# All four down entries of a group ahead of the first chunk in seven products

## The chip, the cores and the metric

The kernel runs on one core of one Trainium2 chip. The core has five engines that run side by side, each with its own in-order list of instructions: TensorE (PE, with its weight loads shown as PEld), VectorE (DVE), ScalarE (ACT), GpSimd (POOL) and SyncE (SP), which issues the loads here. The metric is the device time of one execution in microseconds (us).

## What is computed

The reference is a trunk of two decoder layers on a sequence of 512 tokens of width 1024. Each layer has a gated feed-forward block, a mixer (gated linear attention in layer 0, stick-breaking attention in layer 1) and a second feed-forward block, so that there are four feed-forward blocks (FFNs 1 to 4 below), each with a hidden width of 2816. All in float32.

```python
def swiglu(h, w_gate, w_up, w_down):
    return (jax.nn.silu(h @ w_gate) * (h @ w_up)) @ w_down

for i in range(DEPTH):                                   # DEPTH = 2
    x = x + 0.5 * swiglu(rmsnorm(x, ffn1_norm[i]), ...)  # FFN 1, FFN 3
    x = x + mixer_i(rmsnorm(x, mix_norm[i]))
    x = x + 0.5 * swiglu(rmsnorm(x, ffn2_norm[i]), ...)  # FFN 2, FFN 4
```

## The kernel before

**Numbers as pairs.** Every operand of a matmul is split in two parts: a high part in a shorter format, cast on ACT (`wh`, `hh`, `nh`, `th`), and the rest, the difference on DVE (`wl`, `hl`, `nl`, `tl`). A product is then three matmuls: high by high, low by high, high by low. So each chunk of weights costs, beside its load on SP's queue, one cast on ACT (line 138) and one subtraction on DVE (line 139), and these need free `wh` and `wl` buffers, of which there are four of each.

**Entries and the feed.** The work of TensorE is a list of entries (class `Entry`, line 108), each with the weights that it needs and a body that emits its matmuls and what takes their results. `Feed.start` (line 146) runs the entries in order; before an entry's matmuls it asks for the split of the weights of up to three entries and for the loads of up to six, beginning with its own. What this writes down is an order of the program; a scheduler then orders the instructions of each engine, by its own estimate of times, within what depends on what. Buffers come from pools; a new tile waits for the last user of the buffer that it gets. Raw weights have two buffers (`raw`), raw down weights two of their own (`rawd`).

**An FFN.** Class `FFN` (line 607) cuts the hidden width into 11 chunks of 256 columns, and the chunks into six groups, `GROUPS` in line 614: (0, 1), (2, 3), (4, 5), (6, 7), (8), (9, 10). A group's hidden tiles (two tiles of 128 rows for each chunk; t, cut into `hh` and `hl` by `close`) are multiplied by the down weights later, among the entries of the next group.

- Chunks 0 and 1 use plain products (`feat`, tile `ps_f`), a gate and an up entry for each half chunk, eight entries. The last two call `evac_u` (lines 853 and 854) for the last hidden tiles.
- From chunk 2 on (`SEVEN` = 2) gate and up are made by `seven` (line 684) in seven products of half size in place of eight, with sums and differences of the weight's quarters (tiles `s`, lines 694, 695, 700 and 701, on DVE) and of the input's. Each is two entries, with tiles `ps_w`, `ps_q` and `ps_z`. Seven groups of 12 matmuls of 256 columns follow each other: w, q, w again, z, and then w, q and w once more. Between the first and the third, ACT must copy `ps_w` to `ps_z` (line 736), since the third goes on in `ps_w`. Later ACT copies u from `ps_w` (line 754), DVE adds it (line 755) and adds to the second half (line 759), and for a gate ACT takes the silu (line 719).
- Below, G2 is the gate of chunk 2 in seven products, U2 its up, and so on; each has 84 matmuls.
- The input's sums (`sums`, line 833) are eight pieces of a cast to `th` (ACT, line 806) and a low part `tl` (DVE, line 807). They are spread over the entries that come before G2.
- The down entries of a group are made by `down` (line 312, tile `ps_d`, 24 matmuls of 512 columns). Those of the first group, chunks 0 and 1, are called D0 to D3 here, one for each 256 output columns; each ends in two additions to x on DVE (line 339). D0 is told `late`: it multiplies the three hidden tiles that are there first, and the fourth last. Groups 1 and 3 have their down products in seven as well (`seven_down`, lines 348 and 384).

**Where D0 to D3 stand.** The constructor of `FFN` lays out the list. At the start of group 1 it puts the first `AHEAD` of the four down entries (line 615: `NORMED, SEVEN, AHEAD = 6, 2, 2`), and the others between the entries of the group:

```python
                if group == 1:
                    for put in range(self.AHEAD):
                        down(*downs[put], late=put == 0)
                    put = self.AHEAD
                ...
                    while c >= self.SEVEN and put < len(downs) * (i + 1) // slots:
                        down(*downs[put])
                        put += 1
```

So the list was: eight entries of chunks 0 and 1, D0, D1, G2, U2, G3, D2, U3, D3, G4, U4 and so on. `sums_by`, the place of G2 in the list, is worked out from it, and `run` (line 902) spreads the first five of the sums' pieces over the entries from the seventh to G2, with `spread(todo[:5], self.sums_by - self.NORMED)`; the rest come behind the first entry of G2.

Of the kernel before, what the change touches and what calls it, by code (L numbers as in the profile page):

```python
# [46 lines left out]
def decoder(ctx: ExitStack, tc: tile.TileContext, a: dict, out: bass.AP):  # L47
# [559 lines left out]
    class FFN:  # L607
# [4 lines left out]


        GROUPS = ((0, 2), (2, 4), (4, 6), (6, 8), (8, 9), (9, 11))
        NORMED, SEVEN, AHEAD = 6, 2, 2
        DOWN_SEVEN = (1, 3)
        SEVEN_UP = (2, 3, 4, 5, 6, 7, 8, 9, 10)

# [698 lines left out]
    class SB:  # L1317
# [5 lines left out]
        AHEAD = 5  # L1323
# [582 lines left out]
```

## Time and profile before

| | |
|---|---|
| median of 3 runs | 1781.29 us (1780.68 to 1782.69) |
| the profiled execution | 1780.26 us, its span 1778.3 us |
| TensorE busy | 1760.1 us, 99% of the span, 12714 matmuls |
| weight loads (PEld) busy | 1631.7 us, 92% |
| VectorE busy | 1538.5 us, 87% |
| ScalarE busy | 1050.5 us, 59% |
| granted clock of TensorE | 1.000 |
| DMA | 179.24 MB, mean 101 GB/s |

A row of a timeline gives the start in us from the span's beginning, the duration, the engine, the line, the operation and its tiles (out<-in), the shape and how many were merged; in brackets stands the idle time of the engine before it and what ended it. Matmuls overlap each other, and their ends are modelled: what a matmul costs is read from the distance of the starts, not from its duration. The rows of the waits give who waited for whom, the total in us, the times and the longest. In the first FFN D0 begins at about 54 us and G2 at 64 us; G2 begins at about 611 us in FFN 2, 936 us in FFN 3 and 1497 us in FFN 4.

### The profile page before, as it was taken

How to read it: one execution, taken by the hardware profiler on the slowest of the kernel's cores; microseconds unless marked ns; L12 is line 12 of the kernel's file. 1: busy time of each engine (PE TensorE's matmuls, PEld its weight loads, DVE VectorE, ACT ScalarE, POOL GpSimd, SP SyncE). 2: the span in 40 equal slices, each digit the busy share in tenths (PEclk: the TensorE clock that was granted, in tenths of full speed). 3: DMA queues.
4: the chain of work that ended last, by engine and by line, in shares of the span. 5: the costliest groups of instructions: out<-in, count | busy, mean ns of one | idle time of the engine just before them, and what ended most of it. 6: DMA issues, size and time to landing. Idle time of an engine off the chain costs nothing.

```text
span 1778.3 us, 31182 instructions
## 1 busy us (share of the span) xinstructions
PE 1760.1 (99%) x12714; PEld 1631.7 (92%) x12714; DVE 1538.5 (87%) x2527; ACT 1050.5 (59%) x1830; POOL 9.8 (1%) x24
## 2 busy tenths in 40 slices
PE   9999999999999999999999999999999999999998
PEld 8999999889888899999889999999888888999997
DVE  8999798786878999889798988977898679998986
ACT  7556455554655556555555555655888755565554
POOL 0000000100000000000000000000000000000000
PEclk9999999999999999999999999999999999999999
DMA  5433334322122333333333333322212233333331
GB/s 167 142 115 112 107 96 132 93 71 72 49 95 95 104 110 119 107 107 108 109 93 119 96 119 103 124 84 83 83 48 72 71 95 119 110 105 111 105 126 52
DMA packets 178755, 179.24 MB, mean 101 GB/s; under 512 B 4082, under 2 KB 170276, under 8 KB 178612
## 3 DMA queue, kind: packets, MB, share of 16 engines
q1 hardware_dynamic: 177760, 175.91, 31.6%
q8 instruction: 99, 1.62, 0.4%
q0 software_dynamic: 608, 1.05, 0.2%
q14 instruction: 44, 0.36, 0.1%
q10 hardware_dynamic: 244, 0.29, 0.0%
HBM read 175.17 MB, written 2.10 MB: 100 GB/s over the span
## 4 chain that ended last, share of the span: by engine, by line
PE 64%; DVE 25%; ACT 7%; issue 3%; DMA 1%; SPq 0%; DVEq 0%; ACTq 0%
PE ps_w L709 14%; PE ps_d L80 12%; PE ps_f L80 8%; DVE wl L139 7%; PE ps_q L709 7%; PE ps_t L80 5%; PE ps_z L709 3%; PE ps_b L80 3%; ACT wh L138 3%; PE ps_w L384 2%; DVE x L390 2%; DVE ts L816 1%; PE ps_q L384 1%; PE ps_z L1394 1%; DVE xn L800 1%
## 5 line engine op out<-in xcount | busy, mean ns | idle before, releaser
L139 DVE TENSOR_TENSOR wl<-raw,wh 128x1024 fp32r<-128x1024 f32 x241 | 254.9, 1058 | 58.1 <-ACT wh L138 57.5
L138 ACT CAST wh<-raw 128x1024 fp32r<-128x1024 f32 x241 | 221.6, 920 | 72.4 <-PE ps_f L80 21.5
L139 DVE TENSOR_TENSOR wl<-s,wh 128x1024 fp32r<-128x1024 f32 x176 | 214.2, 1217 | 42.2 <-ACT wh L138 41.9
L138 ACT CAST wh<-s 128x1024 fp32r<-128x1024 f32 x176 | 184.2, 1047 | 102.9 <-DVE s L701 25.7
L709 PE MATMUL ps_w<-th,wh 128*128 128x256 f32 x864 | 239.8, 278 | 3.7 <-ACT ps_z L736 2.7
L709 PE MATMUL ps_w<-th,wl 128*128 128x256 f32 x864 | 237.6, 275 | 0.0
L709 PE MATMUL ps_w<-tl,wh 128*128 128x256 f32 x864 | 237.6, 275 | 0.0
L709 PEld LDWEIGHTS ps_w<-th,wh 128*128 128x128 f32 x864 | 165.8, 192 | 7.4 <-ACT ps_z L736 7.1
L80 PE MATMUL ps_f<-xh,wh 128*128 128x512 f32 x432 | 166.8, 387 | 0.9 <-DVE x L260 0.9
L709 PEld LDWEIGHTS ps_w<-tl,wh 128*128 128x128 f32 x864 | 165.9, 192 | 0.0
L709 PEld LDWEIGHTS ps_w<-th,wl 128*128 128x128 f32 x864 | 165.8, 192 | 0.0
L80 PE MATMUL ps_f<-xh,wl 128*128 128x512 f32 x432 | 164.2, 380 | 0.5 <-DVE wl L139 0.5
L80 PE MATMUL ps_f<-xl,wh 128*128 128x512 f32 x432 | 164.0, 380 | 0.0
L80 PE MATMUL ps_d<-hl,wh 128*128 128x512 f32 x416 | 158.0, 380 | 0.9 <-DVE hl L807 0.8
L80 PE MATMUL ps_d<-hh,wh 128*128 128x512 f32 x416 | 157.7, 379 | 0.2 <-ACT hh L806 0.2
L80 PE MATMUL ps_d<-hh,wl 128*128 128x512 f32 x416 | 157.7, 379 | 0.0
L138 ACT CAST wh<-rawd 128x1024 fp32r<-128x1024 f32 (+1 forms) x100 | 82.9, 845 | 60.1 <-PE ps_d L80 45.2
L139 DVE TENSOR_TENSOR wl<-rawd,wh 128x1024 fp32r<-128x1024 f32 (+1 forms) x100 | 95.7, 961 | 14.7 <-ACT wh L138 14.7
L80 PEld LDWEIGHTS ps_f<-xh,wh 128*128 128x128 f32 x432 | 81.7, 189 | 12.1 <-DVE x L260 1.3
L80 PEld LDWEIGHTS ps_f<-xl,wh 128*128 128x128 f32 x432 | 81.7, 189 | 11.5
L80 PEld LDWEIGHTS ps_f<-xh,wl 128*128 128x128 f32 x432 | 81.7, 189 | 11.1 <-DVE wl L139 0.9
L339 DVE SCALAR_TENSOR_TENSOR x<-ps_d,x 128x512 f32<-128x512 f32 x120 | 79.8, 682 | 13.8 <-PE ps_d L80 13.7
(352 smaller groups left out, 5247.9 us busy)
## 6 DMA issues: line engine op xcount, KB each, us to landing
raw<-in_ffn_w_gate_dram SPq DMA_DIRECT2D x43, 1024.0 KB, 5.4
raw<-in_ffn_w_up_dram SPq DMA_DIRECT2D x43, 1024.0 KB, 5.3
rawd<-in_ffn_w_down_dram SPq DMA_DIRECT2D x84, 512.0 KB, 3.6
raw<-in_gla_w_in_dram SPq DMA_DIRECT2D x12, 1024.0 KB, 5.3
raw<-in_sb_w_in_dram SPq DMA_DIRECT2D x16, 512.0 KB, 3.7
raw<-in_gla_w_out_dram SPq DMA_DIRECT2D x4, 1024.0 KB, 5.2
raw<-in_sb_w_in_dram SPq DMA_DIRECT2D x4, 1024.0 KB, 5.0
raw<-in_sb_w_out_dram SPq DMA_DIRECT2D x4, 1024.0 KB, 5.1
```

The source lines that it names most:

```text
L80: st["pe"] = nc.tensor.matmul(ps, l, r, start=first, stop=last).ins
L138: st["cut"] = nc.scalar.copy(h[:, k], part).ins
L139: nc.vector.tensor_tensor(out=l[:, k], in0=part, in1=h[:, k].bitcast(F32), op=ALU.subtract)
L339: nc.vector.scalar_tensor_tensor(out=x, in0=flat(ps), scalar=0.5, in1=x, op0=ALU.mult, op1=ALU.add)
L384: st["pe"] = nc.tensor.matmul(ps, l_, r_, start=first and c + n == 0, stop=c == 1 and n == 2, skip_group_check=True).ins
L390: nc.vector.scalar_tensor_tensor(out=x, in0=ps, scalar=0.5, in1=x, op0=ALU.mult, op1=ALU.add)
L709: st["pe"] = nc.tensor.matmul(o, l_, r_, start=first and j + n == 0, stop=j == 3 and n == 2, skip_group_check=True).ins
L800: nc.vector.scalar_tensor_tensor(out=t, in0=xs[k], scalar=g, in1=st["R"], op0=ALU.mult, op1=ALU.mult)
L816: nc.vector.tensor_tensor(out=o, in0=p, in1=q, op=ALU.subtract)
L1394: nc.tensor.matmul(o_, l_, r_, start=first, stop=last, skip_group_check=True)
```

## The change

`AHEAD` becomes 4, in the one class that all four FFNs use. All four down entries D0 to D3 stand ahead of G2; the loop among group 1's entries then has none left to put. `sums_by` becomes 12 where it was 10, and so the first five pieces of the input's sums are spread over six entries where it was four. Nothing is added or taken away: each engine has the same instructions in another order.

```diff
         GROUPS = ((0, 2), (2, 4), (4, 6), (6, 8), (8, 9), (9, 11))
-        NORMED, SEVEN, AHEAD = 6, 2, 2
+        NORMED, SEVEN, AHEAD = 6, 2, 4
         DOWN_SEVEN = (1, 3)
```

## The prediction

> **What bounds the kernel now.** I read the page first (busy shares), then busy time by stage, then the waits, then the starts of the matmuls, and last what ACT and DVE did ahead of each late start. The names D0 to D3, G2, U2, G3, U3, G4, U4 are those of the section on the kernel.
>
> ```profile
> 42.00:64.00 22.00, 21.93 (x100) 18.26 (x99) 22.00 (x34) 9.85 (x15) 0.00 (x0) 1.00 0.45 144
> 84.00:113.00 29.00, 29.00 (x218) 27.71 (x217) 26.86 (x46) 16.89 (x30) 0.00 (x0) 1.00 0.39 123
> PEld ps_w L709 <- ACT ps_z L736: 7.1, 18, 1.4
> ```
>
> The first two rows are stages of the first FFN: up to the first seven products, and from G3 to U3. The columns are length, then PE, PEld, DVE, ACT, POOL with their counts, the granted clock, the DMA share and GB/s. TensorE is busy in 21.93 of 22.00 and 29.00 of 29.00 us, at the full clock (1.00). So only starts that come late can be won or lost: the change removes no matmul. In the first stage DVE is busy 22.00 of 22.00 us: it works off the sums' splits and is second to PE. The last row, from the waits, names what holds PE in the seven products: the copy of `ps_w` into `ps_z` on ACT, 18 times.
>
> **What a late start costs, and where.** In a seven-product entry PE forms w, then q, then adds to w; ACT must have copied w to z by then. The last q and the first w of each place in the stretch that changes:
>
> ```profile
> 76.40 0.28 PE L709 MATMUL ps_q<-th,wl 128*128 128x256 f32 x1
> 76.52 0.28 PE L709 MATMUL ps_q<-tl,wh 128*128 128x256 f32 x1
> 76.95 0.38 PE L709 MATMUL ps_w<-th,wh 128*128 128x256 f32 x1 [0.16 <-ACT ps_z L736]
> 77.17 0.28 PE L709 MATMUL ps_w<-th,wl 128*128 128x256 f32 x1
> ...
> 124.82 0.28 PE L709 MATMUL ps_q<-tl,wh 128*128 128x256 f32 x1
> 125.26 0.38 PE L709 MATMUL ps_w<-th,wh 128*128 128x256 f32 x1 [0.16 <-ACT ps_z L736]
> ...
> 623.51 0.28 PE L709 MATMUL ps_q<-tl,wh 128*128 128x256 f32 x1
> 623.77 0.38 PE L709 MATMUL ps_w<-th,wh 128*128 128x256 f32 x1
> ...
> 671.64 0.28 PE L709 MATMUL ps_q<-tl,wh 128*128 128x256 f32 x1
> 672.08 0.38 PE L709 MATMUL ps_w<-th,wh 128*128 128x256 f32 x1 [0.16 <-ACT ps_z L736]
> ...
> 948.12 0.28 PE L709 MATMUL ps_q<-tl,wh 128*128 128x256 f32 x1
> 949.58 0.38 PE L709 MATMUL ps_w<-th,wh 128*128 128x256 f32 x1 [1.19 <-ACT ps_z L736]
> ...
> 1499.14 0.28 PE L709 MATMUL ps_q<-tl,wh 128*128 128x256 f32 x1
> 1499.68 0.38 PE L709 MATMUL ps_w<-th,wh 128*128 128x256 f32 x1 [0.26 <-ACT ps_z L736]
> ```
>
> Undisturbed starts are 0.11 apart (76.40 to 76.52). The wait at 76.95 pushes the start by 0.43 - 0.11 = 0.32, and the next one by 0.22 - 0.11 = 0.11 more: 0.43 lost for 0.16 of idle time. The same reading gives, by place: U2 0.43 (FFN 1), 0.26 (FFN 2), 1.46 (FFN 3), 0 (FFN 4), in all 2.15; G2 in FFN 4 0.54; U4 0.43 in FFN 1 and 0.44 in FFN 2, in all 0.87. U3, which today follows D2, shows none. The places where a U follows its G directly are the ones that lose. Why, in the worst one:
>
> ```profile
> 946.38 0.42 ACT L719 ACTIVATE o<-o 128x256 f32<-128x256 f32 x1 [2.94 <-DVE o L755]
> 948.22 1.03 ACT L138 CAST wh<-s 128x1024 fp32r<-128x1024 f32 x1
> 949.15 0.37 ACT L736 COPY ps_z<-ps_w 128x256 f32<-128x256 f32 x1
> ...
> 944.20 1.21 DVE L139 TENSOR_TENSOR wl<-raw,wh 128x1024 fp32r<-128x1024 f32 x1
> 945.93 0.41 DVE L755 TENSOR_TENSOR o<-u,o 128x256 f32<-128x256 f32 x1
> ```
>
> ACT had copied G2's u by 943.44 (946.38 less its idle 2.94), but DVE came to its add (L755) only at 945.93, being behind with splits and sums; ACT, in its written order, stood idle 2.94 us for it, and the z copy of U2 came last of all, at 949.15.
>
> **The change, part by part.**
>
> *TensorE's order.* In the built program each of the four FFNs now has D0 D1 D2 D3 G2 U2 G3 U3 G4, where it had D0 D1 G2 U2 G3 D2 U3 D3 G4; nothing else moves on PE, and the matmuls are the same. Work itself: 0. A down entry is 24 matmuls of 512 columns, 0.21 apart (1490.75 to 1490.96 in the fence on D0), 5.2 us; the two that move give DVE and ACT 10.4 us more before G2, and take these out of the run behind it.
>
> *DVE and ACT in front of G2.* D2's and D3's casts and splits and their four adds to x come earlier: 2 splits at 1.13 and 4 adds at 0.60 (spacing of the starts below) are 4.7 us of DVE for 10.4 us of PE. DVE thus gains 5.7 us on PE by the start of G2.
>
> So the late L755 at G2 goes away: in the new DVE order no sum or split that isn't needed by then stands directly ahead of it, and what stands ahead is finished while D3 runs. U2 loses between 0 and 0.43 (its smaller rows); I take 0, since the lag that made it is covered: -2.15. G2 of FFN 4 was late for the same lag: -0.54.
>
> *U3 and U4.* U3 now follows G3 directly, with the closing of U2 and one sum ahead of L755 on DVE: the same neighbours as U4 behind G4. Bounds: 0 (its own rows today) and 1.46 (U2 of FFN 3). Walking DVE down from G3's start (cuts of U2's output, 4.4 us; two sums 1.2; splits 0.6, 1.1, 1.1; a sum 0.6) L755 comes 9.1 us after it, when u has waited since 7.2, and z ends 2.72 us behind U3's start, where PE wants it at 2.68. Nearest is the row at 623.77: 0.26. Four times: +1.04. U4 keeps its neighbours: its 0.87 stays; bounds 0 and 4 x 0.44.
>
> *The last h of chunk 1, in D0.* D0 ends on the fourth hidden tile, whose cast (hh, ACT) and low part (hl, DVE) stand amid the moved splits.
>
> ```profile
> 1486.83 0.68 DVE L854 TENSOR_TENSOR t<-ps_f,t 128x512 f32<-128x512 f32 x1
> 1487.43 1.21 DVE L139 TENSOR_TENSOR wl<-s,wh 128x1024 fp32r<-128x1024 f32 x1
> ...
> 1489.69 0.68 DVE L807 TENSOR_TENSOR hl<-t,hh 128x512 fp32r<-128x512 f32 x1
> ...
> 1488.29 0.38 PE L80 MATMUL ps_d<-hl,wh 128*128 128x512 f32 x1
> 1488.90 0.48 PE L80 MATMUL ps_d<-hh,wh 128*128 128x512 f32 x1 [0.23 <-ACT hh L806]
> 1489.22 0.38 PE L80 MATMUL ps_d<-hh,wl 128*128 128x512 f32 x1
> 1490.43 0.48 PE L80 MATMUL ps_d<-hl,wh 128*128 128x512 f32 x1 [0.83 <-DVE hl L807]
> 1490.75 0.38 PE L80 MATMUL ps_d<-hh,wh 128*128 128x512 f32 x1
> 1490.96 0.38 PE L80 MATMUL ps_d<-hh,wl 128*128 128x512 f32 x1
> ...
> 56.44 0.68 DVE L807 TENSOR_TENSOR hl<-t,hh 128x512 fp32r<-128x512 f32 x1
> 58.12 0.38 PE L80 MATMUL ps_d<-hl,wh 128*128 128x512 f32 x1
> ...
> 604.68 0.68 DVE L807 TENSOR_TENSOR hl<-t,hh 128x512 fp32r<-128x512 f32 x1
> 605.42 0.48 PE L80 MATMUL ps_d<-hl,wh 128*128 128x512 f32 x1
> ...
> 929.29 0.68 DVE L807 TENSOR_TENSOR hl<-t,hh 128x512 fp32r<-128x512 f32 x1
> 930.02 0.48 PE L80 MATMUL ps_d<-hl,wh 128*128 128x512 f32 x1
> ```
>
> A short DVE instruction holds the engine 0.60 (1486.83 to 1487.43), a 1024-wide split 1.13 (two of them from 1487.43 to 1489.69). Counting these down the new order from the split of U1's weights, hl starts in FFN 1 1.10 later than today (its reader at 58.12 had 1.00 to spare): +0.25 with the restart. FFN 2: 0.64 earlier, where today the reader starts 0.06 behind hl's end, so waits for it: -0.3. FFN 3: 0.49 later with 0.05 to spare: +0.6. FFN 4: the same instant (two splits of D2 and D3 for the two of G2): 0. Together +0.55; bounds -1.8 (all of it hidden, with FFN 4's 0.4 + 1.0) and +2.4 (as FFN 4 in all).
>
> *Queues and waits.* D2's and D3's loads stand on SP's queue right behind U2's, as today; the next two, the down weights of the following stage, now pass G3's and wait for the splits of D2 and D3 (about 59 us), before G2's raw buffer comes free for G3's load (about 68). G3 is used at 94. No cost. The adds of D2 and D3 on DVE wait for PE; what is queued behind them is for U2 and later, more than 9 us off. On ACT hh now stands behind the cast of D2 (FFN 1, 2) or of D2 and D3 (FFN 3, 4), which wait for their loads:
>
> ```profile
> 51.84 2.71 SPq L105 DMA_DIRECT2D rawd<-in_ffn_w_down_dram  x2
> rawd<-in_ffn_w_down_dram SPq DMA_DIRECT2D x2, 512.0 KB, 3.9
> ```
>
> D0's split comes two short instructions (1.2 us) earlier, and so does the load: in FFN 4 D3's is issued at about 1483.35, lands 3.9 later at 1487.25, its cast ends by 1488.3, hh by 1488.9, the instant of today (0.61 after 1488.23 by the order). 0, with 1 us per FFN as the bound.
>
> [...]
>
> **Sum.** -2.15 - 0.54 + 1.04 + 0.55 = -1.1 us. The profiled execution took 1780.26 (span 1778.3): 1779.2 of its kind. The median of the runs is 1781.29, so 1780.2. A change within 0.2% (3.6 us) is about what a measurement of this kernel can't tell from none.
>
> **The rivals.**
> (1) Faster: ACT and DVE, with 5.7 us in hand, are never late again: U3 and U4 lose nothing and D0's end is hidden. -2.15 - 0.54 - 0.87 - 0.3 - 1.4 (FFN 4) = -5.3: 1776.0. For it: DVE works 22.00 of 22.00 where it would gain. Against: U4 loses 0.44 now, long after that stretch, and hl's place in the order.
> (2) Slower: without D2 and D3 between them G2, U2, G3, U3 starve DVE: it is busy 26.86 of 29.00 us even with the two entries there. If L755 comes 2.5 us behind u at U3, as it did at 945.93, each FFN pays 1.46: -2.15 - 0.54 + 0.55 + 5.84 = +3.7: 1785.0. It decides from some 2.2 us of lag on; I walked to 1.9.
> (3) The loads of D3 land late and hold hh. At one more than the row, 4.9 us, FFN 3 and 4 lose 0.8 each: 1781.8, still no change. It decides only past 7 us, against 3.9 measured. [...]
>
> **Chances.** The forecast 0.62, rival 1 0.16, rival 2 0.14, rival 3 0.08 (within 0.2% too): faster 0.16, same 0.70, slower 0.14. The range goes from -2.15 - 0.54 - 0.87 - 0.3 - 0.4 (U2, G2, U4, and of D0 what FFN 2 and the first wait of FFN 4 lose) = -4.3: 1777.0, to U2 and U3 at 0.43 in every FFN with D0 at its upper end, -2.15 - 0.54 + 3.44 + 2.4 = +3.1: 1784.4, and leaves out about 1 in 10 on each side.
>
> **What would show it.** Right: the wait of PE on `ps_z` at U2 of FFN 3 (1.19) is gone; U3 shows starts 0.2 to 0.4 late; DVE isn't full in the 10 us ahead of G2; hl of FFN 3 keeps D0 waiting some 0.5. Wrong: idle time on ACT ahead of the cast of D2 or D3 with PE waiting for hh; waits for `wl` or `wh` in U2 to U3; U3 waiting over 1 us.

## The result, and the profile after

The changed kernel takes 1790.08 us, the median of 5 runs (1787.10 to 1791.06), against 1781.35 before: a ratio of 1.0044, 95% interval 1.0033 to 1.0056. On another chip it took 1788.36 (1786.70 to 1789.11) against 1780.85: 1.0041, 1.0028 to 1.0054. It is slower by 7.5 to 8.7 us, where I forecast 1780.2 and a range up to 1784.4.

Three kinds of rows show it at once. First the waits of the changed kernel (engine, line, tile, for whom; us in total, times, the longest), then the same groups in the kernel before.

```profile
PE ps_w L709 <- ACT ps_z L736: 3.5, 8, 0.8
PE ps_d L80 <- DVE hl L807: 2.5, 4, 0.6
PE ps_w L384 <- ACT ps_z L402: 2.0, 5, 0.5
PE ps_d L80 <- ACT hh L806: 1.1, 1, 1.1
ACT wh L138 <- DMA rawd<-in_ffn_w_down_dram: 22.0, 13, 5.0
```

```profile
PE ps_w L709 <- ACT ps_z L736: 2.7, 9, 1.2
PE ps_d L80 <- DVE hl L807: 0.8, 1, 0.8
PE ps_d L80 <- ACT hh L806: 0.2, 1, 0.2
ACT wh L138 <- DMA rawd<-in_ffn_w_down_dram: 3.0, 6, 1.0
```

TensorE now waits for `hl` or `hh` in D0 of every FFN, and in a place that wasn't on my list at all: the seven-product down entry of chunks 2 and 3 (line 384, SD0 below), which comes right behind U4 and for which the list of before has no row. ACT waits 22.0 us for the loads of down weights, where it waited 3.0. Two stages of the first FFN of the changed kernel, and behind them G4 and U4 of the kernel before (length; then busy time of PE, PEld, DVE, ACT and POOL, granted clock, DMA share, GB/s):

```profile
44.00:66.00 22.00, 21.28 (x95) 17.31 (x94) 21.44 (x33) 10.74 (x16) 0.00 (x0) 1.00 0.61 191
118.00:135.00 17.00, 16.43 (x147) 16.24 (x146) 17.00 (x28) 10.88 (x22) 0.00 (x0) 1.00 0.25 81
```

```profile
113.00:132.00 19.00, 18.84 (x169) 18.65 (x168) 18.97 (x31) 11.04 (x21) 0.00 (x0) 1.00 0.28 89
```

Before G2 TensorE has 0.7 us of idle time in 22, and DVE, which was to gain there, stands idle 0.56. From 118 to 135 us (most of G4, and U4) DVE is full, 17.00 of 17.00. It was as good as full there before (18.97 of 19.00), so the busy time alone doesn't tell the two kernels apart; how far DVE lags does, as shown under U4.

**Where the time went, in numbers.** The matmuls up to D0 and from G4 on stand in the same order in both kernels. So the distance between the starts of the same two matmuls tells what a stretch costs, whatever was moved within it. These rows, of the kernel before and then of the changed kernel's second profile, are the first matmul of G4, of SD0 and of the entry behind SD0:

```profile
112.88 0.27 PE L709 MATMUL ps_w<-nh,wh 128*128 128x256 f32 x1
...
132.06 0.28 PE L384 MATMUL ps_w<-nh,wh 128*128 128x256 f32 x1
...
141.65 0.28 PE L709 MATMUL ps_w<-nh,wh 128*128 128x256 f32 x1
```

```profile
113.10 0.28 PE L709 MATMUL ps_w<-nh,wh 128*128 128x256 f32 x1
...
132.69 0.28 PE L384 MATMUL ps_w<-nh,wh 128*128 128x256 f32 x1
...
143.25 0.28 PE L709 MATMUL ps_w<-nh,wh 128*128 128x256 f32 x1
```

G4 and U4 took 19.18 and take 19.59 (+0.41); SD0 took 9.59 and takes 10.56 (+0.97). In the same way, against the kernel before, summed over the four FFNs (us):

| kernel | D0 to U3 | G4, U4 | SD0 | sum | profiled execution less 1780.26 |
|---|---|---|---|---|---|
| changed (second profile) | +2.25 | +2.67 | +2.94 | +7.9 | +8.1 |
| cuts_first | -2.89 | +2.70 | +2.94 | +2.8 | +3.0 |
| three_ahead | -0.36 | +0.22 | +0.01 | -0.1 | +0.1 |
| sums_in_four | +0.54 | +2.70 | +2.95 | +6.2 | +6.5 |
| d2_before_u2 | -0.16 | +0.22 | +0.06 | +0.1 | +0.4 |
| u2_load_behind | -1.65 | +2.68 | +2.92 | +4.0 | +4.5 |
| less_dve_work | +3.04 | -0.16 | +2.10 | +5.0 | +3.7 |
| cuts_first_three_ahead | -3.47 | +0.24 | -0.08 | -3.3 | -0.4 |
| covers_one_earlier | +0.17 | +0.51 | +2.93 | +3.6 | +3.9 |
| covers_behind_u3 | +0.47 | +0.58 | -1.58 | -0.5 | -0.9 |

All but 0.2 of the 8.1 us that the changed kernel loses lie in these three stretches. In other kernels the rest of the program differs by up to 1.3 us, and in cuts_first_three_ahead by 2.9. The first profile of the changed kernel (1790.98) and that of cuts_first_three_ahead have some 1.5 us more at the very start of the program; the last section comes back to that.

**D0 to U3.** The first FFN, changed kernel (first profile), ACT, then DVE, then PE:

```profile
53.03 0.62 ACT L806 CAST hh<-t 128x512 fp32r<-128x512 f32 x1 [0.72 <-DVE t L854]
57.81 1.06 ACT L138 CAST wh<-rawd 128x1024 fp32r<-128x1024 f32 x1 [4.17 <-DMA rawd<-in_ffn_w_down_dram]
58.77 0.61 ACT L806 CAST hh<-t 128x512 fp32r<-128x512 f32 x1
...
56.46 0.68 DVE L854 TENSOR_TENSOR t<-ps_f,t 128x512 f32<-128x512 f32 x1
58.90 1.22 DVE L139 TENSOR_TENSOR wl<-rawd,wh 128x1024 fp32r<-128x1024 f32 x1 [0.56 <-ACT wh L138]
60.05 0.68 DVE L807 TENSOR_TENSOR hl<-t,hh 128x512 fp32r<-128x512 f32 x1
...
60.78 0.48 PE L80 MATMUL ps_d<-hl,wh 128*128 128x512 f32 x1 [0.65 <-DVE hl L807]
```

The hidden tile t was ready at 57.14, but ACT stood idle 4.17 us for D2's load with the cast of D2 at the head of its order; `hh` came behind it, and `hl` behind D2's split on DVE. TensorE waits 0.65.

**U4.** The same FFN, ACT, then DVE, then PE:

```profile
122.15 0.37 ACT L754 COPY u<-ps_w 128x256 f32<-128x256 f32 x1 [0.65 <-PE ps_w L709]
125.36 0.42 ACT L719 ACTIVATE o<-o 128x256 f32<-128x256 f32 x1 [0.84 <-DVE o L755]
126.62 1.03 ACT L138 CAST wh<-s 128x1024 fp32r<-128x1024 f32 x1
127.56 0.37 ACT L736 COPY ps_z<-ps_w 128x256 f32<-128x256 f32 x1
...
124.31 0.69 DVE L368 TENSOR_TENSOR s<-rawd 128x512 f32<-128x512 f32 x1
124.91 0.42 DVE L755 TENSOR_TENSOR o<-u,o 128x256 f32<-128x256 f32 x1
...
127.14 0.28 PE L709 MATMUL ps_q<-tl,wh 128*128 128x256 f32 x1
127.98 0.38 PE L709 MATMUL ps_w<-th,wh 128*128 128x256 f32 x1 [0.57 <-ACT ps_z L736]
```

The same two instructions in the kernel before, ACT, then DVE:

```profile
119.83 0.37 ACT L754 COPY u<-ps_w 128x256 f32<-128x256 f32 x1 [1.01 <-PE ps_w L709]
...
121.58 0.42 DVE L755 TENSOR_TENSOR o<-u,o 128x256 f32<-128x256 f32 x1
```

G4's u has been there since 122.52, and DVE adds it at 124.91, 2.4 us late. This is the picture that the prediction showed for U2 of FFN 3 (L755 at 945.93), now at U4 of all four FFNs: the lag is 2.4 us in each, where it was 1.4 (FFNs 1 and 2) and 0.8 (FFNs 3 and 4). What stands ahead on DVE is the closing of U3 (the subtractions of line 877 and the cuts behind them). It began 5.3 us ahead of G4's start while D3 stood there, and now begins 0.4 us behind it, in all four.

### The profile page after: what moved, and what is told of

Read it like the earlier page. It is cut to its first block, busy times and chain, and to the rows that moved or that the text cites. A ratio compares the mean times of both kernels' runs of the same rounds, so it can differ in the third digit from the quotient of the medians.

```text
span 1789.0 us, 31199 instructions
## 1 busy us (share of the span) xinstructions
PE 1764.1 (99%) x12714; PEld 1634.2 (91%) x12714; DVE 1540.3 (86%) x2527; ACT 1053.0 (59%) x1830; POOL 9.8 (1%) x24
## 4 chain that ended last, share of the span: by engine, by line
PE 63%; DVE 25%; ACT 7%; issue 3%; DMA 2%; DVEq 0%; ACTq 0%; SPq 0%
PE ps_d L80 13%; PE ps_w L709 13%; PE ps_f L80 8%; DVE wl L139 8%; PE ps_q L709 6%; PE ps_t L80 5%; PE ps_z L709 3%; PE ps_b L80 3%; PE ps_w L384 3%; ACT wh L138 2%; DMA rawd<-in_ffn_w_down_dram 2%; DVE x L390 2%; PE ps_z L1394 1%; PE ps_q L384 1%; DVE nl L807 1%
## 5 line engine op out<-in xcount | busy, mean ns | idle before, releaser
L80 PEld LDWEIGHTS ps_d<-hl,wh 128*128 128x128 f32 x416 | 78.7, 189 | 15.1 <-DVE hl L807 4.1
```

Source lines behind the costliest of these rows:

```text
L80: st["pe"] = nc.tensor.matmul(ps, l, r, start=first, stop=last).ins
```

## The experiments

The theory after the result has two causes. (a) D2's and D3's casts and splits stand ahead of the last `hh` and `hl` on ACT and DVE and wait for loads. (b) Without D2 and D3 between the chunks DVE falls behind, and U4 and SD0 pay. The rivals are named in the expectations.

### The casts behind the cut, the order of TensorE kept

```diff
-                e.split()
+                with (tc.issue_after(st["hh"]) if e.wait else ExitStack()), (tc.issue_after(st["hl"]) if e.wait else ExitStack()): e.split()
...
                         down(*downs[put], late=put == 0)
+                        feed.q[-1].wait = put > 1
...
-            self.hs[group].append(self.cut(h, l, t))
+            self.hs[group].append(self.cut(h, l, t)); st["hh"], st["hl"] = st["closed"], st["low"]
```

> The changed kernel, with the order of TensorE, the loads and the sums as they are; only the casts and splits of D2's and D3's weights are put behind the cut (hh on ACT, hl on DVE) of the last hidden tile that D0 ends on. Theory (two causes: these casts wait for late loads and hold hh and hl, and DVE falls behind in six seven-product entries in a row): D0's late starts were 5.0 us in all after the change and fall to about 0.5, the rest stays, so 4.5 us less than the changed kernel, about 1785.6. Rival 1 (DVE's backlog alone makes the loss, and what D0 saves comes back as later waits): within 1 us of the changed kernel, 1789 to 1791. Rival 2 (D0's end alone makes the loss): 1781 to 1782.

Measured: 1783.83 (1.0014, 1.0005 to 1.0022). The first stretch goes from +2.25 to -2.89, while U4 and SD0 stay at +2.70 and +2.94 to 0.03 us. So both rivals fall: what D0 saves (5.1) isn't lost again, and D0 isn't the whole. ACT in the first FFN:

```profile
55.38 0.62 ACT L806 CAST hh<-t 128x512 fp32r<-128x512 f32 x1 [3.53 <-DVE t L854]
55.91 1.04 ACT L138 CAST wh<-rawd 128x1024 fp32r<-128x1024 f32 x1
57.66 1.05 ACT L138 CAST wh<-rawd 128x1024 fp32r<-128x1024 f32 x1 [0.71 <-DMA rawd<-in_ffn_w_down_dram]
```

`hh` now waits for its tile and for nothing else. The saving is 0.6 above the 4.5 expected: I had counted the late starts without the 0.1 that the start behind each one loses.

### Is it the loads, or the casts themselves?

```diff
-                nc.sync.dma_start(self.t, self.src)
+                with tc.issue_after(st["rawd"]) if self.behind else ExitStack(): st["rawd" if self.few else "raw"] = nc.sync.dma_start(self.t, self.src).ins
```

(`behind` is set for the up weights of chunk 2.)

> The changed kernel, with the load of U2's weights (1 MB) put behind those of D2 and D3 on SP's queue, ahead of which it stands; ACT's order is the same. Theory, in the form that the late loads of D2 and D3 are what makes the casts hold hh: these loads land about 1 us sooner (3.5 to 3.9 us after issue, not 4.6 to 4.9), and D0 loses some 2.5 us less over the four FFNs: 1788 - 2.5 = 1785.5. In the form that the order of the casts, and their own 1.0 us on ACT and 1.1 on DVE, is what holds them, whenever the loads land: no more than 1 us less, 1787 to 1788.

Measured: 1784.27 (1.0020, 1.0010 to 1.0029). From issue to landing the down loads take 3.6 us, where the changed kernel's second profile has 4.9, both between 42 and 62 us (KB each, median us to landing):

```profile
rawd<-in_ffn_w_down_dram SPq DMA_DIRECT2D x4, 512.0 KB, 3.6
```

```profile
rawd<-in_ffn_w_down_dram SPq DMA_DIRECT2D x4, 512.0 KB, 4.9
```

The first stretch falls by 3.9 with ACT's order unchanged, so it is the late landing that does most of it. D2's load, issued as far ahead of D0 as in the changed kernel, lands 1.7 to 3.0 us sooner, more than the 1 us that I expected, and the time is 1.2 below my 1785.5. What D0 still loses beyond the first experiment's order (1.2 us) lies in FFNs 3 and 4, where casts and splits of D2 and D3 still stand ahead of `hh` and `hl`. DVE's order moved a little too (sums behind the splits), so not every tenth of the 3.9 is the load's.

### D3 back between U3 and G4

```diff
-        NORMED, SEVEN, AHEAD = 6, 2, 4
+        NORMED, SEVEN, AHEAD = 6, 2, 3
```

> Three entries ahead, and D3 between U3 and G4. Theory: D3 gives DVE 5.2 us of TensorE's time to catch up before G4, so the late starts of U4 (3.3 us in all after the change) and of the seven-product down entry behind it (4.0) go back to those of before (0.65 and 0.8), 5.9 us less; D2's cast still stands ahead of hh, so most of D0's loss stays, 1 us less; in all about 1783.2. Rival 2 (D0's end alone): U4 and what is behind it stay late, and the time is 1788 to 1790 or falls only by D0's 1 to 2 us. Rival 3 (the sums' pieces, spread over six entries where there were four, make the loss, here over five): half of it, about 1785.7.

Measured: 1780.58 (0.9998, 0.9989 to 1.0007), better than expected. U4 and SD0 are back at +0.22 and +0.01, with one entry of 5.2 us put back; rival 2 falls again. That the first stretch (-0.36) came out 1.6 below what I reckoned has most of its cause in FFN 4, where D3's cast no longer stands ahead of `hh`: D0 loses 0.5 there, where the changed kernel loses 2.3.

### The sums spread as before

```diff
-                spread(todo[:5], self.sums_by - self.NORMED)
-                feed.entries(1, True)
+                spread(todo[:5], 4)
+                feed.entries(self.sums_by - self.NORMED - 4), feed.entries(1, True)
```

> The changed kernel with the sums' first five pieces spread over four entries, as in the kernel before, instead of six. Theory: the order of TensorE and the casts is that of the changed kernel, so within 1.5 us of it: 1788.5 to 1791.5. Rival 3 (the spread of the sums makes the loss): 1780 to 1783.

Measured: 1787.08 (1.0031, 1.0019 to 1.0043), 1.3 below the changed kernel and below the interval that I gave. U4 and SD0 don't move. The first stretch does, by 1.7; FFN 4 alone gains 1.86, and there `hh` now comes ahead of D3's cast. The spread of the sums isn't the cause; it shifts the same order on ACT.

### Another place for D2, D3 behind U3

```diff
-        NORMED, SEVEN, AHEAD = 6, 2, 4
+        NORMED, SEVEN, AHEAD = 6, 2, 2
...
-                    while c >= self.SEVEN and put < len(downs) * (i + 1) // slots:
+                    while c >= self.SEVEN and put < ((3, 3, 3, 4)[i] if group == 1 else len(downs) * (i + 1) // slots):
```

> D0 and D1 ahead as in the kernel before, D2 between G2 and U2, D3 between U3 and G4. Theory: no cast holds D0's last h, every G but G3 has a down entry or its own U apart, so U2's late starts go (-2.15 of before), U3 pays 0.28 in each FFN (+1.1), U4 pays nothing (-0.65): 1781.35 - 1.7 = 1779.7. Rival 1 (a place without cover ahead of the U chunks costs as in the changed kernel): over 1784. Rival 3 (only the sums matter, which are spread as before): 1781.3.

Measured: 1780.63 (0.9997, 0.9988 to 1.0006), 0.9 above the expected: U2's late starts went, but G2 of FFN 1 has a new one of 0.97, and U3 pays 1.6 in all, not 1.1. Rival 1 (over 1784) falls. Rival 3's 1781.3 can't be told from the theory by this run; the one before has answered it.

### Which closings have to be covered

Two more places, with `(3, 3, 4, 4)` (D2 before U2, D3 before U3) and with `(2, 2, 2, 4)` (D2 and D3 behind U3) in the line above.

> D0 and D1 ahead, D2 between G2 and U2, D3 between G3 and U3, so that U3, G4 and U4 follow each other without a down entry, as in the changed kernel, while both entries still stand in the stretch and no cast of theirs stands ahead of D0's last h. Theory (a backlog of DVE: what counts is how much of TensorE's time without closings and sums has gone by since DVE fell behind): DVE gets the 5.2 us of D3 before the closing of U3, not behind it, and U4 loses 0.4 to 0.9 in each FFN and the down entry behind it some 0.3: 1782 to 1784. Rival (neighbours decide, as the prediction took it: U4 stands behind G4 as in the kernel before): U4 loses the 0.33 of before in the first two FFNs and nothing in the others, 1780 to 1781.

> D0 and D1 ahead, G2 U2 G3 U3 without a down entry, then D2 and D3, then G4 U4. Theory (backlog): U2 as in the kernel before (2.15 in all); U3 late by 0.3 to 1.5 in each FFN, as four entries in a row stand ahead of it with only D0 and D1 before; U4 and the entry behind it as before or better: 1782 to 1785. Rival (neighbours decide): U3 0.28 in each FFN, 1781.5 to 1782.

Measured: 1784.03 (1.0019, 1.0010 to 1.0029) and 1779.43 (0.9993, 0.9983 to 1.0003). With D3 before U3, SD0 loses 2.93, as much as in the changed kernel, and U4 0.51, where the changed kernel has 2.68: neighbours don't decide, since U4 stands behind G4 in all of these kernels. The time lies at the upper end of the theory's range, but in part by luck. U4 is late by 0.31 to 0.45 in each FFN, at the low end of what I expected, while SD0 is late by 0.8 to 1.6, where I had 0.3; and G3 of FFNs 1 and 2, with D3 right behind it, loses 1.08 each, which no run here explains and which takes back what U2 gains.

With D2 and D3 behind U3, U4 and SD0 lose nothing together (+0.58 - 1.58). But here the theory failed as I had put it: U3, with four entries in a row, was to lose 0.3 to 1.5 in each FFN, and loses 0.32 in the first and 0.05 in each of the others. So the first four entries don't make the debt. The reading that fits all the places tried is that DVE falls behind with the closing of U3, and that SD0 needs a down entry between U3 and G4: one entry earlier, D3 saves SD0 nothing. U4 is helped by that earlier place too.

### Less work for DVE

```diff
-            sub(2, o1[:, H:T], o0[:, H:T])
-            sub(3, o1[:, 0:H], ts[:, 1])
...
+            b["t3"], b["t4"] = b["t1"], b["t2"]
```

(The branch that cuts t3 and t4 goes. So the kernel leaves out a part of every closing of a seven-product group, that of chunks 6 and 7 too.)

> The changed kernel, which leaves out part of the closing of the chunks of a seven-product group: two of four subtractions (sub 2 and sub 3) and the cut of t3 and t4, for which t1 and t2 are used again; TensorE does as many matmuls as before. That is about 1.3 us less on DVE and 0.6 on ACT for each of U2 and U3. Theory (DVE's backlog makes U4 and the seven-product down entry behind it late): the 5.6 us that they lose more than in the kernel before go, D0's loss stays: 1788 - 5.6 = about 1782.5, 1781 to 1784. Rival (they are late for another reason, loads or PSUM buffers): 1787 to 1789.

Measured: 1782.27 (1.0008, 0.9999 to 1.0018). U4's loss is gone (-0.16, where it was +2.67): there it is the amount of work in the closings, on DVE and, by the 0.6 us of each cut, on ACT. Its third group of products starts 0.22 after the last q:

```profile
125.26 0.28 PE L709 MATMUL ps_q<-tl,wh 128*128 128x256 f32 x1
125.48 0.38 PE L709 MATMUL ps_w<-th,wh 128*128 128x256 f32 x1
```

SD0 keeps 2.10 of its 2.94, so the theory is only half right there: 3.7 of the 5.6 us went. That the time lies in the theory's range all the same is in part luck, since the rest of the program is 1.3 us shorter than before. What SD0 waits for are these rows on ACT and DVE of the changed kernel's first profile (SD0 starts at 134.78):

```profile
136.26 0.62 ACT L806 CAST hh<-o 128x512 fp32r<-128x512 f32 x1 [1.52 <-DVE o L722]
136.78 1.06 ACT L138 CAST wh<-s 128x1024 fp32r<-128x1024 f32 x1
137.75 0.61 ACT L402 COPY ps_z<-ps_w 128x256 f32<-128x256 f32 x2
...
134.53 0.69 DVE L694 TENSOR_TENSOR s<-raw 128x512 f32<-128x512 f32 x1
135.14 0.42 DVE L759 TENSOR_TENSOR o<-ps_q,o 128x256 f32<-128x256 f32 x1
```

A sum for a later chunk (L694) stands between U4's last additions, and a cast of U4's output and one of weights stand ahead of SD0's z copies. Before, that sum was done ahead of the additions (L755 at 130.88, L759 at 131.67), and `hh` started 0.5 us after SD0, not 1.5. covers_one_earlier has this order of U4's additions to 0.02 us (L755 0.58 and L694 0.25 ahead of SD0's start, L759 0.36 behind it) and the same loss, though U4 loses little there; three_ahead has them as before (L755 1.17 ahead) and loses no more than before. In the run with less work L694 no longer stands between the additions, but another sum (L695) stands ahead of them: L755 starts 0.55 ahead, `hh` 1.15 behind. So SD0's loss goes with how late U4's additions come. That the order of the sums, beside the amount of work, makes them late is read from these rows; no run moved a sum alone.

### Both causes taken away, and the changed kernel once more

```diff
-        NORMED, SEVEN, AHEAD = 6, 2, 4
+        NORMED, SEVEN, AHEAD = 6, 2, 3
```

(on top of the first experiment's edit)

> Three entries ahead, D3 between U3 and G4, and D2's cast and split put behind the cut of D0's last hidden tile. Theory (the two causes are separate and add up): of the late starts of the run with three ahead, D0's 0.35 + 1.06 + 1.39 + 0.19 = 3.0 us go, 1780.6 - 3.0 = 1777.6, faster than the kernel before by 3.6. Rival (what D0 saves is lost again in DVE's backlog by U3 or U4): 1780 to 1781.

> The changed kernel once more, on the chip of the other runs. Its profiled execution of 1790.98 showed 1.5 us at the start of the program (starts 0.43 apart, where the others show 0.22, from 7.3 to 10.3 us), which the change doesn't touch. Theory: that belongs to single executions; here the first 41 us cost what they cost in the kernel before, and the median is 1787.5 to 1789. If it belongs to the changed program, 1790 again, with the same starts in its first 41 us.

Measured: 1778.03 (0.9985, 0.9977 to 0.9994), faster than both kernels, by 2.8 and 10 us. The causes add up: -3.47 in the first stretch is three_ahead's -0.36 less 3.1. The changed kernel once more: 1788.36, with the usual first 41 us.

## Why the prediction was wrong

Step by step, against the 7.9 us measured in the three stretches, where the sum was -1.1:

- **U2 and G2, -2.69: right, and 0.4 short.** No late start is left at either place, and by the mechanism forecast: G2's L755 came 0.2 to 2.5 us behind u and now comes 0.03 behind it in all four FFNs. The gain is 3.1, since G2 of FFN 1 had lost another 0.41, in small late starts that the sum doesn't have. One sign did not come: in the 10 us ahead of G2 DVE is as full as before (10.00 of 10.00 in FFN 1). U2 of FFN 3, which lost 1.46, now starts w 0.11 after the last q:

```profile
966.58 0.28 PE L709 MATMUL ps_q<-tl,wh 128*128 128x256 f32 x1
966.69 0.28 PE L709 MATMUL ps_w<-th,wh 128*128 128x256 f32 x1
```

- **U3, +1.04: right in kind, a little small.** The walk down DVE's order gave a lag of 1.9 us behind u, and it is 1.95; the price that I took from the nearest row was 0.26 in each FFN. It is 0.38 (0.28, and 0.10 at the next start), the same in all four: 1.5. In the first FFN:

```profile
108.00 0.28 PE L709 MATMUL ps_q<-tl,wh 128*128 128x256 f32 x1
108.39 0.38 PE L709 MATMUL ps_w<-th,wh 128*128 128x256 f32 x1
```

- **D0's last h, +0.55, and the loads, 0: wrong, 3.8 in their place** (D0's late starts come to 5.9 us, where they came to 2.1). I counted DVE's instructions and took D2's and D3's loads at 3.9 us after issue. In the changed kernel's second profile they take 4.6 to 6.6, since U2's 1 MB load is issued only 1.7 us ahead of them on the queue (50.72 and 52.46 in the first FFN of the first profile; 48.90 and 51.84 before); with that load put behind them they take 3.4 to 4.2. So the cast of D2 waits, and `hh` and `hl` wait behind it: the idle time on ACT ahead of that cast, which the prediction named as a sign of being wrong. The mechanism stood in the text, as a bound of 1 us per FFN and as the third rival. Beyond what I forecast D0 loses 0.4, 1.6, 0.6 and 0.7 in FFNs 1 to 4, 3.3 in all: within four times the bound, though FFN 2 is past it. But I took its value as 0, gave the rival 0.8 each in FFN 3 and 4 only, said that it decides only past 7 us, and left its 4 us out of the range. The upper end for D0, 2.4, was low too: both waits of FFN 4 (0.4 + 1.0) in the other three, less the 0.3 that FFN 2 has already, are 3.9.
- **The two premises of the third rival, ACT's order and the load's time.** The first was right: on ACT `hh`, whose tile was ready at 57.14, starts at 58.77, behind D2's cast at 57.81, for which ACT had stood idle 4.17 us. The second, 3.9 us, was too low: in the first FFN D2's and D3's loads take 3.4 and 3.7 with the 1 MB load behind them (u2_load_behind), and 4.6 to 5.3 with it just ahead.
- **U4, unchanged: wrong, +2.67.** "U4 keeps its neighbours" was the step that failed. The runs show that not the neighbours count but what DVE owes from U3's closing: with D3 back between U3 and G4 the loss is 0.22, with less work in the closings it is gone.
- **SD0: not in the sum, +2.94.** I followed the change as far as U4 and no further. D3's place between U3 and G4 is what kept SD0 from losing (three_ahead, +0.01; with D3 one entry earlier 2.93 stays). That it did so by keeping DVE's sums for the next chunks ahead of U4's additions is read from the rows above.

The sizes that failed add up: 3.3 in D0, 5.6 in U4 and SD0 and 0.5 in U3, less the 0.4 more that G2 gave, are the 9.0 us between -1.1 and +7.9. Rival 2 had the right mechanism (DVE starved without D2 and D3 between the chunks, L755 more than 2.2 us behind u), at the wrong chunk: the lag at U3 was small, and the 2.4 us came at U4. Rivals 2 and 3 came true together. I had given them 0.14 and 0.08 as alternatives and nothing to both, and the range held neither rival 2's 1785.0 nor four times the bound of rival 3.

## What to carry to other kernels

When an entry that is light for the second-busiest engine is moved away, look for the loss not only where it stood but two or three entries behind the heavy closing that it covered: there the debt came due here (U4 and SD0, two and three entries behind U3, +2.67 and +2.94), and following the engine's order that much further would have shown it. A cast moved ahead in ACT's order brought its load's landing time with it here (4.17 us of idle ACT in the first FFN, with `hh` behind it), and the price of that load was the one behind what stood ahead of it on the queue (4.6 to 5.3 us in the first FFN, the 1 MB load issued 1.7 ahead), not the median of the kernel before (3.9, the 1 MB load 2.9 ahead). A cost that is bounded by 1 us in four places belongs in the range with all 4.

## What the hardware showed that I hadn't expected

**Half speed behind short waits.** In the run with less work for DVE, D0 of FFN 4 waits twice within 2 us, and then the matmuls of 512 columns start 0.43 apart, not 0.22, for some 3 us, with the granted clock at 0.50 (PE rows, then the busy time of two stretches with the clock behind the five engines):

```profile
1490.93 0.48 PE L80 MATMUL ps_d<-hh,wh 128*128 128x512 f32 x1 [1.17 <-ACT hh L806]
1492.27 0.48 PE L80 MATMUL ps_d<-hl,wh 128*128 128x512 f32 x1 [0.64 <-DVE hl L807]
1493.78 0.63 PE L80 MATMUL ps_d<-hh,wh 128*128 128x512 f32 x1
1494.20 0.64 PE L80 MATMUL ps_d<-hh,wl 128*128 128x512 f32 x1
```

```profile
1490.00:1493.00 3.00, 1.43 (x5) 0.91 (x6) 2.61 (x4) 0.88 (x2) 0.00 (x0) 0.95 0.61 179
1493.00:1496.00 3.00, 3.00 (x9) 2.37 (x8) 2.56 (x4) 1.04 (x1) 0.00 (x0) 0.50 0.55 171
```

Eight starts at 0.21 too much are 1.7 us, more than either wait, and more than half of this kernel's +3.04 in the first stretch; the profiled execution (1783.97) is 1.7 above the kernel's median. In both profiles of the changed kernel the same two waits (1.3 and 0.8 late) were not followed by it: in the first, a stretch with 1.26 us of work in 3 holds them, and the starts behind it are 0.22 apart, at a clock of 1.00. In the run with less work a stretch with 1.43 us in 3 was followed by it once. What decides whether it comes is not shown by any run.

**The start of the program.** In the first profile of the changed kernel, and in that of cuts_first_three_ahead, the matmuls from 7.3 to 10.3 us start 0.43 apart as well; in the other profiles they don't. It costs those executions 1.5 us, about 1.8 by the time of D0, and lies ahead of everything that the change moves; the changed kernel's second profile doesn't have it. The granted clock of that stretch reads 1.00, so the distance of the starts told it, not the clock:

```profile
8.16 0.63 PE L1697 MATMUL ps_f<-xh,wl 128*128 128x512 f32 x1
8.58 0.63 PE L1697 MATMUL ps_f<-xl,wh 128*128 128x512 f32 x1
```

```profile
7.30:10.50 3.20, 3.20 (x9) 2.39 (x8) 2.77 (x7) 2.32 (x6) 0.00 (x0) 1.00 1.12 346
```
